# An encoder layer on one core: the last 512 tokens' down projection by seven block products

## The chip, the cores and the metric

The kernel runs on one core of a Trainium2 chip. The metric is the device time of one execution in microseconds (us). A core has a matrix engine (PE, with a separate stream PEld for loading stationary operands), a vector engine (DVE), a scalar engine (ACT), a third elementwise engine (POOL) and a queue engine (SP) that mostly issues transfers (DMAs) between the memory of the chip (HBM) and the core's own memories: SBUF for operands and PSUM, eight banks of 128 partitions x 512 floats, in which matmuls accumulate. Every engine works through its own instructions in order and waits on semaphores.

## What is computed

One layer of a hybrid encoder on 2048 tokens of width 1024 in float32; in front of the part that changes stand an attention over a dilated window, a convolution and a cross-attention. The projection of the values `v` is part of `w_in`; the MLP and the last norm are what the change is about.

```python
D_MODEL, SEQ, D_FF = 1024, 2048, 4096
y = rmsnorm(h, norm_mix_g[l]) @ w_in[l]            # q, k, v and the convolution's a, g
v = y[..., 2 * D_ATT:3 * D_ATT].reshape(B, S, ATT_HEADS, HEAD_DIM)
h = h + jnp.concatenate([att, conv], axis=-1) @ w_out[l]
...
h = h + xo @ w_xo[l]                               # cross-attention
u = rmsnorm(h, norm_mlp_g[l]) @ w_up[l]
h = h + jnp.square(jax.nn.relu(u)) @ w_down[l]
return rmsnorm(h, norm_final_g)
```

## The kernel before

**Numbers.** Every float32 operand of a matmul is split into a high part, rounded to the form that PE takes, and a low part, the rest. A product is three matmuls, high x high, low x high and high x low (`mm3`, L199 to L201). For weights, `wsplit2` does the split: ACT copies the raw tile to the high part (L190), DVE subtracts for the low part (L191). A weight tile of 512 KB (128 x 1024 floats) is loaded through `dma` (L57) on SP's queue into one of two buffers "raw"; there are four pairs of split buffers.

**Stages.** The first 540 us make projections; the last of these is `lin_v` (L548 on), in two rounds of two heads' groups: the raw weights times a scale (L560, DVE), cast (L562, ACT), low part (L563, POOL), then matmuls of 256 columns into PSUM, taken out by ACT (L574) and DVE (L575, `vst`), and stored to HBM (`vtok`). `weave` interleaves it with a convolution (`conv0`) on DVE. Then four passes of 512 tokens follow, p = 0 to 3; in each, `post(p)` makes the output projection, the cross-attention, the MLP and the final norm, with attention and convolution of the next pass woven in as sides. The last pass has no sides.

**The MLP of a pass.** h stays in SBUF transposed: eight tiles `hs[m]` of 128 features x 512 tokens. The 4096 hidden features come in eight groups (`fg`) of 512. In a group, four "up" steps c = 0 to 3 each make 128 hidden features x 512 tokens from one weight tile: 8 x 3 matmuls of 128x512. DVE takes the maximum with zero and the norm's scale (`rl`, L1321), ACT squares (L1322) and casts (`hhh`, L1323), DVE makes the low part (`hhl`, L1324). Four "down" steps follow, each with one weight tile (4 x 128 hidden features x 256 outputs) and two outputs' blocks of 4 x 3 matmuls of 128x512, added to `hs[m]` by DVE (L1339). So a group has 96 matmuls up and 96 down. Weights are the stationary operand in both, tokens the moving one. Up and down share three PSUM banks.

**The end.** In the last group of the last pass the down steps run on 256 tokens at a time (192 matmuls of 128x256), with squares summed beside them (`add_sq`, L1164, L1165). `final` takes the norm's factor (a matmul with ones `nps`, L1174; DVE L173; a power on POOL, L177; three DVE steps L178 to L180), multiplies by the gain (`fin`, L1360), turns blocks of 128x128 with PE (`ot`, L1367), scales on the way out of PSUM (L1369 on ACT, L1371 on DVE) and stores each half row block.

The order in which instructions stand on each engine is made by a scheduler from the program's order, from what `weave` interleaves and from priorities (`pinned`).

Of the kernel before, what the change touches and what calls it, by code (L numbers as in the profile page):

```python
# [10 lines left out]
F32 = mybir.dt.float32  # L11
# [36 lines left out]
def hybrid_layer(ctx, tc, A, out):  # L48
# [70 lines left out]
    bscr = dr.tile([KC, P, KC, P], F32, name="bscr")  # L119

# [77 lines left out]
    def mm3(o, lh, ll, rh, rl, first, end):  # L198
        PE.matmul(o, lh, rh, start=first, stop=False)  # L199
        PE.matmul(o, lh, rl, start=False, stop=False)  # L200
        last["pe"] = PE.matmul(o, ll, rh, start=False, stop=end)  # L201
# [1017 lines left out]
    def post(p):  # L1219
# [88 lines left out]
        end = p == NG - 1  # L1308
        for fg in range(FG):
# [16 lines left out]
            if fg == FG - 1:  # L1326
                fsum = ssum_tile(f"f{p}")
                if not end:
                    load_cat(p + 1, 0)

            def down(mp2, t, w, wh, wl):
                sl = slice(t, t + w)
                for e in range(2):
                    m = 2 * mp2 + e
                    es = slice(P * e, P * e + P)
                    pt = ps("mm", "dn")[:, 0:w]
                    for k in range(4):
                        mm3(pt, wh[:, k, es], wl[:, k, es], hh["h", k][:, sl], hh["l", k][:, sl], k == 0, k == 3)
                    last["dve"] = DVE.tensor_tensor(hs[m][:, sl], hs[m][:, sl], pt, op=ALU.add)  # L1339
                    if fg == FG - 1:  # L1340
                        add_sq(hs[m][:, sl], fsum[:, sl], m == 0)

            wd = []
            for mp2 in range(4):
                wd.append(wpost(wcols(w_down, mp2 * 256, 256, (4 * fg, 4 * fg + 4)), f"d{p}{fg}_{mp2}", (P, 4, 256)))
                if fg == FG - 1 and end:
                    continue
                down(mp2, 0, 512, *wd[-1])
                yield


        fin = {}

        def final(t, w):
            r = rstd_from(fsum[:, t:t + w])
            sl = slice(t, t + w)
            for k in range(KC):
                if t == 0:
                    fin[k] = ytile("h", k, f"fin{p}_{k}", F32)
                DVE.tensor_scalar(fin[k][:, sl], hs[k][:, sl], gain("final", k), None, op0=ALU.mult)  # L1360
            for j in range(w // P):
                c0 = t + P * j
                for g in range(2):
                    ot = ytile("l", 2 * (c0 // P) + g, f"ot{p}{c0}{g}", F32)
                    pt = ps("T", "ot")
                    for i in range(4):
                        PE.transpose(pt[:, P * i:P * i + P], fin[4 * g + i][:, c0:c0 + P], ident)  # L1367
                    if g:
                        ACT.activation(ot, pt, AF.Copy, scale=r[:, j:j + 1])  # L1369
                    else:  # L1370
                        DVE.tensor_scalar(ot, pt, r[:, j:j + 1], None, op0=ALU.mult)  # L1371
                    dma(out[0, 512 * p + c0:512 * p + c0 + P, 512 * g:512 * (g + 1)], ot)
                yield

        if end:
            for t in range(0, 512, 256):
                for mp2 in range(4):
                    down(mp2, t, 256, *wd[mp2])
                yield from final(t, 256)
        else:  # L1380
            load_cat(p + 1, 1)
            yield from final(0, 512)

    for p in range(NG):
# [8 lines left out]
        if p + 1 < NG:  # L1393
# [3 lines left out]
            sides = [(att(p + 1), 0.95), (cg, 0.6)]  # L1397
# [60 lines left out]
```

## Time and profile before

| | us |
|---|---|
| median of three runs | 2888.64 |
| lowest, highest | 2881.66, 2890.31 |
| the profiled execution | 2888.26 |
| its span, from the first to the last instruction | 2886.5 |
| busy time of PE in it | 2826.6 (98%) |
| busy time of DVE | 1857.6 (64%) |
| busy time of ACT | 1166.3 (40%) |
| mean granted PE clock | 0.994 |

The profile is of one execution. A row of a timeline has the start and the length in us, the engine, the line, the operation and its tiles, and in brackets the idle time before it and what ended it. A row of a group has the count, the busy time in us, the mean length of one in ns, the idle time before the group's instructions and what ended most of it. A line of the view of windows has, for a stretch, the busy time and count of PE, PEld, DVE, ACT and POOL, then PE's granted clock (1.00 is full), the mean busy share of the DMA engines and the GB/s they moved. A line of the waits has what waited for what, the sum in us, how often, and the longest.

### The profile page before, as it was taken

What the parts mean: (1) busy time and instruction counts of PE and PEld (TensorE: products, weight loads), DVE (VectorE), ACT (ScalarE), POOL (GpSimd) and SP (SyncE); (2) the same over time, 40 slices, a digit from 0 to 9 for tenths busy, and PEclk for the clock granted to TensorE, in tenths of its full rate; (3) what the DMA queues carried; (4) which work ended last, traced back from release to release, by engine and by line L of the source; (5) the groups of instructions that cost most, each with busy time, mean ns of one, the idle gap of its engine ahead of it and who ended that gap; (6) DMA issues with size and microseconds to landing.
All of it is one profiled execution on the core that took longest, in us unless ns stands there. A gap on an engine that the chain in (4) does not pass through costs nothing.

```text
span 2886.5 us, 41313 instructions
## 1 busy us (share of the span) xinstructions
PE 2826.6 (98%) x15628; PEld 2376.2 (82%) x15628; DVE 1857.6 (64%) x3306; ACT 1166.3 (40%) x1988; POOL 458.0 (16%) x469
## 2 busy tenths in 40 slices
PE   8999999998999999999999999999999999999999
PEld 7878899887788888888888888888888888888887
DVE  5636535565789776557887765689876555544445
ACT  5633211475554333434543343444333433432233
POOL 1336421122102011200012012002011200000000
PEclk9999999999999999999999999999999999999999
DMA  8979845799734444554444446534543445333332
GB/s 264 295 173 228 202 132 131 182 256 247 205 102 131 135 133 123 168 160 145 121 130 130 138 117 192 175 96 128 142 127 109 139 132 175 93 90 101 96 95 74
DMA packets 598632, 433.74 MB, mean 150 GB/s; under 512 B 191550, under 2 KB 524786, under 8 KB 597921
## 3 DMA queue, kind: packets, MB, share of 16 engines
q1 hardware_dynamic: 558256, 408.21, 50.2%
q10 hardware_dynamic: 37952, 16.88, 2.4%
q0 software_dynamic: 2224, 6.01, 0.6%
q8 instruction: 123, 2.02, 0.3%
q14 instruction: 77, 0.62, 0.1%
HBM read 339.89 MB, written 91.11 MB: 149 GB/s over the span
## 4 chain that ended last, share of the span: by engine, by line
PE 82%; DVE 9%; DMA 5%; issue 2%; ACT 2%; POOL 1%; SPq 1%; POOLq 0%; DVEq 0%; ACTq 0%
PE dn L199 8%; PE dn L200 8%; PE dn L201 8%; PE up L199 7%; PE up L200 7%; PE up L201 7%; PE lin L199 4%; PE lin L201 4%; PE lin L200 4%; DVE cacc L216 3%; PE o L199 2%; PE o L200 2%; PE o L201 2%; PE xs L199 2%; PE xs L201 2%; PE xs L200 2%
## 5 line engine op out<-in xcount | busy, mean ns | idle before, releaser
L199 PE MATMUL dn<-hhh,whi_d 128*128 128x512 f32 (+1 forms) x1056 | 402.8, 392 | 7.2 <-DVE h L1339 6.1
L200 PE MATMUL dn<-hhl,whi_d 128*128 128x512 f32 (+1 forms) x1056 | 403.4, 385 | 1.1 <-DVE hhl L1324 1.1
L199 PE MATMUL up<-mh,whi_u 128*128 128x512 f32 x1024 | 402.9, 393 | 0.5 <-DVE rl L1321 0.5
L201 PE MATMUL dn<-hhh,wlo_d 128*128 128x512 f32 (+1 forms) x1056 | 402.6, 384 | 0.0
L200 PE MATMUL up<-ml,whi_u 128*128 128x512 f32 x1024 | 399.4, 390 | 1.0 <-DVE ml L1214 0.9
L201 PE MATMUL up<-mh,wlo_u 128*128 128x512 f32 x1024 | 399.7, 391 | 0.0
L216 DVE SCALAR_TENSOR_TENSOR cacc<-cu,cw,cacc 128x512 f32<-128x512 f32 x480 | 389.0, 811 | 5.5
L190 ACT CAST whi_d<-raw_d 128x1024 fp32r<-128x1024 f32 x128 | 134.6, 1052 | 418.1 <-PE up L200 378.6
L1339 DVE TENSOR_TENSOR h<-h,dn 128x512 f32<-128x512 f32 (+1 forms) x264 | 172.3, 667 | 162.9 <-PE dn L201 161.7
L190 ACT CAST whi_u<-raw_u 128x1024 fp32r<-128x1024 f32 x128 | 134.4, 1050 | 327.2 <-PE dn L200 304.1
L1321 DVE SCALAR_TENSOR_TENSOR rl<-up,ssumx 128x512 f32<-128x512 f32 x128 | 88.0, 690 | 256.9 <-PE up L201 252.6
L199 PEld LDWEIGHTS dn<-hhh,whi_d 128*128 128x128 f32 x1056 | 198.1, 189 | 47.5 <-DVE h L1339 10.2
L201 PEld LDWEIGHTS dn<-hhh,wlo_d 128*128 128x128 f32 x1056 | 198.8, 188 | 39.7
L200 PEld LDWEIGHTS dn<-hhl,whi_d 128*128 128x128 f32 x1056 | 199.3, 189 | 37.4 <-DVE hhl L1324 2.0
L200 PEld LDWEIGHTS up<-ml,whi_u 128*128 128x128 f32 x1024 | 192.4, 188 | 40.1 <-DVE ml L1214 2.3
L201 PEld LDWEIGHTS up<-mh,wlo_u 128*128 128x128 f32 x1024 | 192.2, 188 | 40.3
L199 PEld LDWEIGHTS up<-mh,whi_u 128*128 128x128 f32 x1024 | 192.4, 188 | 38.5 <-DVE rl L1321 0.9
L774 ACT ACTIVATE sm<-sm,o 128x256 f32<-128x256 f32 (+1 forms) x384 | 160.1, 466 | 126.3 <-DVE o L773 125.9
L773 DVE CUSTOM_DVE_ANT_0 sm<-s,mask 128x256 f32<-128x256 f32 (+1 forms) x384 | 128.5, 375 | 83.5 <-PE s L999 39.4
L191 DVE TENSOR_TENSOR wlo_u<-raw_u,whi_u 128x1024 fp32r<-128x1024 f32 x128 | 158.4, 1237 | 32.7 <-ACT whi_u L190 32.4
L191 DVE TENSOR_TENSOR wlo_d<-raw_d,whi_d 128x1024 fp32r<-128x1024 f32 x128 | 163.2, 1275 | 23.8 <-ACT whi_d L190 23.7
L177 POOL TENSOR_TENSOR nr<-st_v,mhalf 128x4 f32<-128x4 f32 (+1 forms) x13 | 13.0, 997 | 839.2 <-DVE st_v L173 839.2
(403 smaller groups left out, 6320.9 us busy)
## 6 DMA issues: line engine op xcount, KB each, us to landing
raw_u<-in_w_up_dram SPq DMA_DIRECT2D x128, 512.0 KB
raw_d<-in_w_down_dram SPq DMA_DIRECT2D x128, 512.0 KB
raw_o<-in_w_out_dram SPq DMA_DIRECT2D x32, 512.0 KB
raw_a<-ascr SPq DMA_DIRECT2D x32, 512.0 KB
raw_b<-bscr SPq DMA_DIRECT2D x32, 512.0 KB
k<-kscr SPq DMA_DIRECT2D x24, 512.0 KB
k<-kscr SPq DMA_DIRECT2D x8, 1152.0 KB
xn<-in_x_dram SPq DMA_DIRECT2D x32, 256.0 KB
```

Source lines behind the costliest of these rows:

```text
L177: POOL.tensor_tensor(dst, v, mhalf.to_broadcast([P, v.shape[1]]), op=ALU.pow)
L190: ACT.copy(hi, raw)
L191: (lo_eng or DVE).tensor_tensor(lo, raw, f(hi), op=ALU.subtract)
L199: PE.matmul(o, lh, rh, start=first, stop=False)
L200: PE.matmul(o, lh, rl, start=False, stop=False)
L201: last["pe"] = PE.matmul(o, ll, rh, start=False, stop=end)
L216: DVE.scalar_tensor_tensor(acc, u[:, t:t + 512], cw[:, c, t:t + 1], acc, op0=ALU.mult, op1=ALU.add)
L773: last["dve"] = DVE.tensor_tensor_reduce(dst, so, mask[:, 256 * m:256 * m + nk], 1.0, 3e38, ALU.add, ALU.min, mn)
L774: last["act"] = ACT.activation(dst, dst, AF.Exp, bias=mn, scale=-1.0)
L1321: last["dve"] = DVE.scalar_tensor_tensor(r, pt, 0.0, rsb, op0=ALU.max, op1=ALU.mult)
L1339: last["dve"] = DVE.tensor_tensor(hs[m][:, sl], hs[m][:, sl], pt, op=ALU.add)
```

## The change

In the last pass the function `last_mlp` takes the place of the MLP, and `down_sums` makes sums of weights ahead of it.

- For groups 0 to 6 the down projection is turned: stationary is the hidden activation (128 features x 128 tokens), moving are 512 columns of weights, and the result is 128 tokens x 512 outputs, added by DVE to h kept by rows of tokens. A group's product of (512 tokens x 512 features) with (512 features x 1024 outputs) is cut into 2 x 2 blocks, and seven products of blocks (A11, A12, S2, S1, S3, S4, A22; Winograd's form of Strassen's scheme) take the place of eight. Each is 2 x 2 x 3 = 12 matmuls of 128x512.
- The accumulators X, Y and Z of PSUM are read by DVE after each product that adds to them, and X and Z are accumulated further afterwards (`more`). X has banks 0 and 1, Y and Z share banks 2 and 3, and the up steps get 4 to 7.
- `parts` makes the activations' blocks and their sums S1 to S4, each split in two, on DVE and ACT.
- Of the seven weight tiles of a group, three are read from `w_down` and four, sums of blocks, from `dscr` in HBM, each as two DMAs of 256 KB; with the four up tiles there are eleven tiles a group for eight.
- `down_sums` fills `dscr`: for each of 7 groups, 4 m and 2 j a unit of two loads of 128x256 floats (SP's queue), four DVE subtractions of 128x128 in place, and two stores (ACT's queue). Groups 0 to 3 are woven beside `lin_v`, groups 4 to 6 given to the last pass as a side.
- h is turned into rows during the first two up steps of group 0 (32 transposes, 8 ACT copies); the 32 transposes behind the norm go.
- Group 7 has its down projection by rows without the seven products: for each of four row blocks and two halves 4 x 3 matmuls of 128x512. The first up step of the next group stands ahead of the seven products.
- The final norm goes row block by row block: ACT squares and sums along the row, DVE and POOL make the factor, DVE multiplies by factor and gain in one step (two per row block), and the two halves are stored from SP's and ACT's queue.

```diff
+    dscr = dr.tile([7, 4, P, 4, 256], F32, name="dscr")
...
+    def down_sums(pl, tag, fgs):
+        for fg, m, j in ((fg, m, j) for fg in fgs for m in range(4) for j in range(2)):
+            raw = pl.tile([P, 2, 256], F32, tag=tag, name=f"ds{fg}{m}{j}", bufs=2)
+            for a in range(2):
+                k = 4 * fg + 2 * a + j
+                dma(raw[:, a], w_down[P * k:P * k + P, 256 * m:256 * m + 256])
+            yield
+            (b11, b12), (b21, b22) = ([raw[:, a, P * b:P * b + P] for b in range(2)] for a in range(2))
+            for o, x, y in ((b11, b12, b11), (b12, b22, b12), (b22, b22, b11), (b21, b21, b22)):
+                last["dve"] = DVE.tensor_tensor(o, x, y, op=ALU.subtract)
+            for a in range(2):
+                dma(dscr[fg, m, :, 2 * a + j], raw[:, a], nc.scalar)
...
-        for _ in range(4):
-            next(steps)
-        weave(islice(steps, 8), (conv0, 1))
-        for _ in range(4):
-            next(steps)
+        ds = pinned(down_sums(pool("dsum", stack=st), "ds", range(4)), "dve")
+        weave(islice(steps, 4), (ds, 2))
+        weave(islice(steps, 8), (conv0, 1), (ds, 2))
+        weave(islice(steps, 4), (ds, 2))
+        drain(ds)
         weave(steps, (conv0, 2.2))
...
+    def last_mlp(hs, y, rsb):
+        FG, p = 8, NG - 1
+        banks.update(up=(4, 5, 6, 7), ux=(0, 1), uy=(2, 3), tr=(0, 1, 2, 3))
...
+        def parts(rs_, c):
+            r, j = rs_[c], c % 2
+            lo, hi = r[:, 0:256], r[:, 256:512]
+            if c < 2:
+                split([x[:, j] for x in A1], lo)
+                DVE.tensor_tensor(lo, lo, hi, op=ALU.subtract)
+                split([x[:, j] for x in S3], lo)
+            else:
+                r0 = rs_[j]
+                split([x[:, j] for x in A2], r)
+                DVE.tensor_tensor(r0[:, 256:512], r0[:, 256:512], hi, op=ALU.add)
+                DVE.tensor_tensor(r0[:, 0:256], hi, r0[:, 0:256], op=ALU.subtract)
+                split([x[j] for x in S12], r0)
+                DVE.tensor_tensor(lo, lo, r0[:, 0:256], op=ALU.subtract)
+                split([x[:, j] for x in S4], lo)
+        def seven(fg):
...
+            X, Y, Z = ([ps(kind, "dn") for _ in range(2)] for kind in ("ux", "uy", "uy"))
+            for n, (key, w, pts, more, t0, c0) in enumerate((
+                    ("A11", direct(0, 0), X, False, 0, 0), ("A12", direct(1, 0), Y, False, 0, 0),
+                    ("S2", sums(1, 1), X, True, 0, 1), ("S1", sums(0, 0), Z, False, 2, 1),
+                    ("S3", sums(0, 1), X, True, 2, 1), ("S4", direct(1, 1), Z, True, 0, 1),
+                    ("A22", sums(1, 0), X, True, 2, 0))):
+                raw = wp.tile([P, 2, 512], F32, tag="raw", name=f"raw_d{p}{fg}{n}", bufs=2)
+                for j in range(2):
+                    dma(raw[:, j].rearrange("p (m c) -> p m c", m=4), w[j])
...
+                wh, wl = wsplit2(wq if i % 4 > 1 else wp, raw, f"d{p}{fg}_{n}", shape=(P, 2, 512))
+                for t in range(2):
+                    for j in range(2):
+                        mm3(pts[t], at[key](0, j, t), at[key](1, j, t), wh[:, j], wl[:, j], not more and j == 0, j == 1,
+                            more)
+                    a = row(t0 + t).rearrange("p (m h c) -> p m h c", m=4, h=2)[:, :, c0, :]
+                    last["dve"] = DVE.tensor_tensor(a, a, pts[t].rearrange("p (m c) -> p m c", m=4), op=ALU.add)
+        rs_ = []
+        for fg in range(FG - 1):
+            for c in range(4):
+                if c or not fg:
+                    rs_.append(hidden(fg, c))
+                parts(rs_, c)
+            rs_ = [hidden(fg + 1, 0)]
+            seven(fg)
...
+        for t in range(4):
+            for c in range(2):
+                pt = ps("tr", "dn")
+                for k in range(4):
+                    wh, wl = ws[c][k // 2]
+                    mm3(pt, *(x[:, k, P * t:P * t + P] for x in hh), wh[:, k % 2], wl[:, k % 2], k == 0, k == 3)
+                a = row(t)[:, 512 * c:512 * c + 512]
+                DVE.tensor_tensor(a, a, pt, op=ALU.add)
+                ACT.activation(tmp("sq"), a, AF.Square, accum_out=ss[:, 2 * t + c:2 * t + c + 1])
...
+            rstd_col(r[:, 0:1], sq, 1, top)
+            for c in range(2):
+                a = row(t)[:, 512 * c:512 * c + 512]
+                DVE.scalar_tensor_tensor(a, a, r[:, 0:1], grow[:, 512 * c:512 * c + 512], op0=ALU.mult, op1=ALU.mult)
+                dma(out[0, 512 * p + P * t:512 * p + P * (t + 1), 512 * c:512 * c + 512], a, nc.scalar if c else None)
...
+        else:
+            sides = [(down_sums(kq, "k", range(4, 7)), 1.2)]
         weave(main, *sides)
```

More of the change, by code (lines that the diff above doesn't have):

```diff
@@ L1349, in post @@
                 yield
+        load_cat(p + 1, 1)
+        r = rstd_from(fsum)
         fin = {}
-        def final(t, w):
-            r = rstd_from(fsum[:, t:t + w])
-            sl = slice(t, t + w)
-            for k in range(KC):
[L1358 to L1382, printed above, removed]
+        for k in range(KC):
+            fin[k] = ytile("h", k, f"fin{p}_{k}", F32)
+            DVE.tensor_scalar(fin[k], hs[k], gain("final", k), None, op0=ALU.mult)
+        for j in range(4):
+            c0 = P * j
+            for g in range(2):
+                ot = ytile("l", 2 * j + g, f"ot{p}{c0}{g}", F32)
+                pt = ps("T", "ot")
+                for i in range(4):
+                    PE.transpose(pt[:, P * i:P * i + P], fin[4 * g + i][:, c0:c0 + P], ident)
+                if g:
+                    ACT.activation(ot, pt, AF.Copy, scale=r[:, j:j + 1])
+                else:
+                    DVE.tensor_scalar(ot, pt, r[:, j:j + 1], None, op0=ALU.mult)
+                dma(out[0, 512 * p + c0:512 * p + c0 + P, 512 * g:512 * (g + 1)], ot)
+            yield
```

88 lines of the change are left out of this document (70 added, 18 removed).

## The prediction

> **What bounds the kernel now.** I read the page from the top: span, engines, the chain that ended last; then the last pass by groups of equal shape; then single rows.
>
> ```profile
> span 2886.5 us, 41313 instructions
> PE 2826.6 (98%) x15628; PEld 2376.2 (82%) x15628; DVE 1857.6 (64%) x3306; ACT 1166.3 (40%) x1988; POOL 458.0 (16%) x469
> PE 82%; DVE 9%; DMA 5%; issue 2%; ACT 2%; POOL 1%; SPq 1%; POOLq 0%; DVEq 0%; ACTq 0%
> 2400.00:2700.00 300.00, 298.80 (x1345) 245.79 (x1344) 155.69 (x221) 107.22 (x159) 2.01 (x2) 1.00 0.35 106
> ```
>
> TensorE sets the time: 98% of the span, 298.8 of 300 us in the last pass's MLP (columns of the last line: length, then busy time of PE, weight loads, DVE, ACT, POOL, granted clock, DMA share, GB/s). DVE is busy 52% there and the clock is full. So a matmul less in this stage is time, as long as DVE, ACT and the weight loads keep pace with fewer matmuls.
>
> What is a matmul worth? The grouped rows give a mean of 389 ns, but that is a latency: rows overlap, and the distance of the starts counts.
>
> ```profile
> L200 PE MATMUL dn<-hhl,whi_d 128*128 128x512 f32 x108 | 41.6, 389 | 0.0
> 2835.05 0.39 PE L199 MATMUL up<-mh,whi_u 128*128 128x512 f32 x1
> 2835.28 0.39 PE L200 MATMUL up<-ml,whi_u 128*128 128x512 f32 x1
> ...
> 2837.77 0.39 PE L199 MATMUL up<-mh,whi_u 128*128 128x512 f32 x1
> 2869.24 0.28 PE L200 MATMUL dn<-hhl,whi_d 128*128 128x256 f32 x1
> 2869.36 0.28 PE L201 MATMUL dn<-hhh,wlo_d 128*128 128x256 f32 x1
> ...
> 2869.84 0.60 PE L1367 MATMUL ot<-ident,fin 128*128 128x128 f32 x4
> 2870.19 0.36 PE L199 MATMUL dn<-hhh,whi_d 128*128 128x256 f32 x1
> ```
>
> Twelve starts lie between 2835.05 and 2837.77: 2.72/12 = 0.2267 us for 512 columns. 256 columns take 0.12, four transposes 0.35.
>
> **The term that shrinks.** In groups of hidden features 0 to 6 (of 8), 96 down matmuls become seven products of 12, so 84: 7 x 12 x 0.2267 = **-19.0 us**. (By the 389 ns it would be 32.7, which would be wrong.)
> The Trainium skill, "TensorE: Matmul & The Clock Gate", "Wait — 56ns, not 53.3ns?", has warm matmuls start every 215.7 ns at 512 columns; the measured distance is 5% longer, and by the page the term would be 18.1 us.
>
> **The end of the pass.**
>
> ```profile
> 2850.47 0.39 PE L201 MATMUL up<-mh,wlo_u 128*128 128x512 f32 x1
> 2850.69 0.28 PE L199 MATMUL dn<-hhh,whi_d 128*128 128x256 f32 x1
> ...
> 2878.70 0.70 POOL L177 TENSOR_TENSOR nr<-st_v,mhalf 128x2 f32<-128x2 f32 x1 [10.40 <-DVE st_v L173]
> 2879.43 0.16 DVE L178 TENSOR_TENSOR st_t<-nr 128x2 f32<-128x2 f32 x1 [0.81 <-POOL nr L177]
> ...
> 2882.36 0.75 DVE L1371 TENSOR_SCALAR ot<-ot,nr 128x512 f32<-128x512 f32 x1 [1.59 <-PE ot L1367]
> ```
>
> From the first down matmul of group 7 (2850.69) to the span's end (2886.5) pass 35.8 us: half-width matmuls, 32 transposes, the norm, the output. The last output is ready at 2883.11, so its transfer closes the span 3.4 us later. After the change: 96 x 0.2267 = 21.8 us, then for the last row block an add (0.69), a square with its sum (0.62 and some 0.2, estimated), a sum and a variance (0.16 each), POOL's power (0.81 with its hand-over), three small operations (0.6), two scalings (1.4), 3.4 for the output and some 0.5 of hand-overs: 8.5. Together 30.3: **-5.5**. The 32 transposes are not gone but turn h into rows in group 0: 8 x 0.35 = **+2.8**. Their four banks are emptied by eight ACT copies, and ACT is at 36% there; with the copies late, the second four groups would wait, up to 3 us.
>
> In group 7 the down matmuls now stand right behind the last up:
>
> ```profile
> 2703.51 0.69 DVE L1321 SCALAR_TENSOR_TENSOR rl<-up,ssumx 128x512 f32<-128x512 f32 x1 [3.35 <-PE up L201]
> 2704.24 0.62 ACT L1322 ACTIVATE rl<-rl 128x512 f32<-128x512 f32 x1
> 2704.89 0.62 ACT L1323 CAST hhh<-rl 128x512 fp32r<-128x512 f32 x1
> ```
>
> From rl's start to the end of the split (another 0.69 on DVE) 2.8 to 2.9 us; nine matmuls on earlier features cover 2.0: **+1** (0 to 2).
>
> **The seven products: do the others keep pace?** Per product PE needs 2.72 us. Rows of the same work:
>
> ```profile
> L191 DVE TENSOR_TENSOR wlo_d<-raw_d,whi_d 128x1024 fp32r<-128x1024 f32 x16 | 19.6, 1226 | 2.7 <-ACT whi_d L190 2.7
> L1339 DVE TENSOR_TENSOR h<-h,dn 128x512 f32<-128x512 f32 x28 | 18.7, 686 | 37.2 <-PE dn L201 37.2
> L190 ACT CAST whi_d<-raw_d 128x1024 fp32r<-128x1024 f32 x16 | 16.9, 1054 | 56.0 <-PE up L200 56.0
> L1339 DVE TENSOR_TENSOR h<-h,dn 128x256 f32<-128x256 f32 x16 | 6.6, 420 | 3.3 <-PE dn L201 2.9
> ```
>
> DVE: two adds and one split, 2 x 0.686 + 1.226 = 2.60 of 2.72 us: it just fits, and what is late in the products is caught up in the ups (5.44 us each). Over a whole group DVE has some 22 operations of 512, 14 of 256 and 11 splits: 15.1 + 5.9 + 13.5 = 34.5 of 40.8 us. A PSUM bank that is read between two accumulations is written again only one product later (the order X, Y, X, Z, X, Z, X), so an add may come 2.7 us late before PE stands.
>
> The weights, a load for each 2.72 us instead of 5.44:
>
> ```profile
> 2698.92 1.23 DVE L191 TENSOR_TENSOR wlo_u<-raw_u,whi_u 128x1024 fp32r<-128x1024 f32 x1 [0.17 <-ACT whi_u L190]
> 2703.28 1.05 ACT L190 CAST whi_d<-raw_d 128x1024 fp32r<-128x1024 f32 x1 [4.39 <-PE up L200]
> 2702.50:2703.00 0.50, 0.50 (x4) 0.42 (x3) 0.00 (x0) 0.00 (x0) 0.00 (x0) 1.00 1.02 360
> 2703.00:2703.50 0.50, 0.50 (x4) 0.42 (x3) 0.00 (x0) 0.22 (x1) 0.00 (x0) 1.00 0.26 88
> ```
>
> A raw buffer is free at 2700.15 and its 512 KB are in at about 2703.2, so 3.1 us; with cast and split 5.5 for one of two buffers, 2.75 per weight. That is PE's pace, but four split pairs are full when the products begin, so the last weight is still made some 5 us ahead of its use. I take **+1** for all seven groups (0 to 14, 2 us a group, if DVE's order puts a split behind a waiting add).
>
> **The sums of weights** are what the change pays. 56 units: two loads of 128 KB on SP's queue, four 128x128 subtractions on DVE, two stores from ACT's queue, two buffers. From 0.686 for 512 and 0.420 for 256 elements a subtraction costs an estimated 0.285, a unit 1.14 on DVE; 32 units beside the values' projection make 36.5 us, 24 more 27.4.
>
> In the instruction order of the changed kernel the 24 stand in the third pass (its groups 4 to 6), ahead of the last pass. DVE there:
>
> ```profile
> 2220.00:2240.00 20.00, 20.00 (x116) 16.30 (x115) 16.41 (x26) 8.12 (x13) 7.01 (x6) 1.00 0.34 93
> 2240.00:2260.00 20.00, 20.00 (x109) 16.85 (x109) 9.85 (x18) 7.59 (x12) 1.39 (x1) 1.00 0.36 111
> ```
>
> 26 of 40 us are taken (66%); 27.4 us spread over the some 90 us of three groups add 30%, so DVE is nearly full, and hidden parts stand in its order behind subtractions that wait for loads. I take **+2.5** (0 to 10).
>
> The values' projection is the open place:
>
> ```profile
> 440.00:460.00 20.00, 20.00 (x91) 16.47 (x90) 6.10 (x8) 4.10 (x5) 3.82 (x4) 1.00 0.15 46
> 460.00:480.00 20.00, 20.00 (x164) 19.80 (x163) 12.67 (x20) 3.44 (x8) 7.32 (x8) 1.00 0.78 204
> 388.30 1.21 DVE L560 TENSOR_TENSOR raw_v<-raw_v,vbc 128x1024 f32<-128x1024 f32 x1
> 456.42 1.22 DVE L560 TENSOR_TENSOR raw_v<-raw_v,vbc 128x1024 f32<-128x1024 f32 x1
> 457.67 1.05 ACT L562 CAST wvh<-raw_v 128x1024 fp32r<-128x1024 f32 x1 [5.08 <-DVE raw_v L560]
> 458.79 2.39 POOL L563 TENSOR_TENSOR wvl<-raw_v,wvh 128x1024 fp32r<-128x1024 f32 x1 [3.73 <-ACT wvh L562]
> L199 PE MATMUL v<-wvh,xh x256: 277/283/283, 393.0 to 506.8; 128*128 128x256 f32 x128
> 467.35 0.36 SPq L57 DMA_DIRECT2D vtok<-vst  x1
> 470.82 0.11 POOL L572 MEMSET vst<- 128x8 f16 x1 [1.76 <-DMA vtok<-vst]
> ```
>
> DVE has room (6 to 13 of 20 us), but it works in order, and between the two multiplications of raw_v at 388.30 and 456.42 stand 19 units: each must take no more than 68/19 = 3.6 us, or the second comes late, and behind it ACT's cast, POOL's 2.39 us and the values' matmuls, with no slack. A unit: its load 2.2 to 3.1 us (3.1 for 512 KB above; half of that is the stream), 1.14, its store 2.2 to 3.5 (the 130 KB stored from 467.35 release POOL at 470.82): 5.5 to 7.7 for each of two buffers, 2.8 to 3.9 per unit. Then ten units beside the second half of the projection (its matmuls end at 507), where the DMA engines were 78% busy already, hold up the evacuations (vst) behind them. At 2.8 nothing is lost; at 3.9, 19 x 0.3 + 3. One wait may vanish in exchange:
>
> ```profile
> PE lin L199 <- DVE vst L575: 3.1, 1, 3.1
> ```
>
> I take **+4** (-3 to +9).
> The Trainium skill, "DMA: Bandwidth & Descriptors", speaks against these transfers: "Anatomy of one DMA" gives every DMA about 2.0 us plus bytes at 436 GB/s, most of it the receipt of the write, heaviest in HBM, and "Bandwidth" advises 1 MiB or more. By it, an estimate, a 128 KB transfer takes 2.3 us and a unit 2.9, which is near the lower bound of the rows.
>
> **Sum** against the profiled run, 2888.3 us (1.8 of them outside the span; the median of the runs is 2888.6, 0.3 more): -19.0 - 5.5 + 2.8 + 1 + 1 + 2.5 + 4 = -13.2, **2875 us**.
>
> **Rivals.** (a) *The sums hide wholly*, loads and stores at the lower bounds: without the 6.5, 2868 to 2869; at best, with the 3.1 of the vanished wait, 2865. For it: DVE's idle time; against: waits in order.
> (b) *The sums eat most of the gain*: both places at their upper bounds, +9 and +10 for 6.5, so 2887, between 2880 and 2895. For it: the 78% DMA share from 460 on; against: a late DVE is caught up where PE has several banks ahead.
> (c) *DVE paces the seven products.* An add reads its PSUM and a strided half of a row; if it costs 0.95 instead of 0.69, a product takes 3.13 and not 2.72: 49 x 0.41 = 20 us, 2895 less what the ups catch up, some 2888. It decides from (2.72 - 1.23)/2 = 0.75 us per add. Against: the 128x512 add is 0.686 in 28 cases.
> (d) *Slower than before: the units set the pace of the projection.* If a buffer's cycle is 10 us, because the stores in HBM come back late behind the projection's own traffic, a unit takes 5 us and 32 need 160, where the projection has 120 (388 to 507): +40 for my +4, 2911. Over the bound of 2897 it comes from a cycle of about 9.1 us on; the rows give at most 7.7.
> (e) The change does not do what it says: PE's order shows 84 matmuls per group, so I give it nothing.
>
> **How the numbers follow.** What a measurement of this kernel can tell from no change is about 0.3%, 8.7 us: faster is under 2880, slower over 2897. Chances: the forecast 0.50 (its own range 2869 to 2881), (a) 0.10, (b) 0.20, (c) 0.08, (d) 0.12. Faster: nearly all of the forecast, (a) and a little of (b), 0.62; slower: (d) and the ends of (b) and (c), 0.14; the same 0.24. The range, 2864 to 2893, leaves out (d) and some of the edges.
>
> **What would show it.** Steps: seven groups of 84 matmuls at 0.2267 us, so about 40.8 us per group; the span's end some 30 us behind the last up; no idle PE with an add's or a split's name in the seven; PE waits of the values' projection (about 388 to 510) and of the third pass's last groups longer by 6 or 7 us together, named after vst, wvl, hhl or rl, with subtractions ahead of them on DVE. Wrong it would be if a unit takes over 4 us, if the adds take over 0.75, or if the last pass shows PE waits of more than 2 us in each group.

## The result and the profile after

| | us |
|---|---|
| before, median of 5 runs | 2888.64 |
| after, median of 5 runs (2928.04 to 2938.66) | 2935.26 |
| after, the profiled execution's span | 2936.9 |
| ratio after / before, 95% interval | 1.0165 (1.0143 to 1.0186) |
| forecast, with its range | 2875 (2864 to 2893) |

The change costs 46.6 us where 13 were to be won. The page of the profile after, and its view of PE's waits:

```profile
span 2936.9 us, 41990 instructions
PE 2850.7 (97%) x15440; PEld 2366.5 (81%) x15440; DVE 1999.5 (68%) x3669; ACT 1204.2 (41%) x2055; POOL 455.5 (16%) x471
PE 73%; DMA 11%; DVE 10%; issue 2%; SPq 2%; ACT 1%; POOL 0%; ACTq 0%; DVEq 0%; POOLq 0%
L761 DVE TENSOR_TENSOR ds<-ds 128x128 f32<-128x128 f32 x224 | 80.2, 364 | 96.5 <-DMA ds<-in_w_down_dram 79.8
```

```profile
PE vbc L186 <- DVE raw_v L562: 11.3, 1, 11.3
PE lin L201 <- DVE vst L577: 10.5, 2, 10.2
PE dn L201 <- DVE h L1356: 7.3, 3, 2.5
...
PE dn L202 <- DVE hhl L1343: 5.1, 4, 2.9
```

The chain that ended last now has 11% DMA where it had 5%; the units' subtractions (ds) sat 80 us waiting for their own loads; two waits of over 10 us stand at the values' projection. But one number doesn't fit a story of waits alone: PE has 188 matmuls fewer (15440 for 15628) and is busy 24 us *longer* (2850.7 for 2826.6). The next view is of windows of 200 us in the last pass, before and after:

```profile
2640.00:2840.00 200.00, 200.00 (x880) 164.55 (x879) 94.04 (x111) 58.72 (x72) 0.00 (x0) 1.00 0.33 98
```

```profile
2640.00:2840.00 200.00, 200.00 (x869) 162.92 (x868) 153.96 (x228) 91.03 (x123) 0.00 (x0) 1.00 0.48 140
```

At full clock and with PE busy throughout, 200 us hold 869 matmuls instead of 880. The rows of one up step of the profile after say the same:

```profile
2657.65 0.39 PE L201 MATMUL up<-mh,whi_u 128*128 128x512 f32 x1
2657.88 0.40 PE L202 MATMUL up<-ml,whi_u 128*128 128x512 f32 x1
2658.11 0.39 PE L203 MATMUL up<-mh,wlo_u 128*128 128x512 f32 x1
...
2663.02 0.39 PE L203 MATMUL up<-mh,wlo_u 128*128 128x512 f32 x1
```

From the first of these rows to the last there are 23 distances (from the start of one matmul to the start of the next) in 5.37 us: 0.2335 us where the prediction counted 0.2267. In both profiles I took all distances of 512-column matmuls: from 1000 us on the mean is 227.8 ns before and 231.1 after, and the distances differ by as much between 100 and 370 us, where nothing in the code has changed yet. So there are at least two losses: waits around the sums, and a slower PE in the whole program.

### The profile page after: what moved, and what is told of

The parts are those of the page before. It is cut to its first block, busy times and chain, and to the rows that moved or that the text cites. A ratio compares the mean times of both kernels' runs of the same rounds, so it can differ in the third digit from the quotient of the medians.

```text
span 2936.9 us, 41990 instructions
## 1 busy us (share of the span) xinstructions
PE 2850.7 (97%) x15440; PEld 2366.5 (81%) x15440; DVE 1999.5 (68%) x3669; ACT 1204.2 (41%) x2055; POOL 455.5 (16%) x471
## 4 chain that ended last, share of the span: by engine, by line
PE 73%; DMA 11%; DVE 10%; issue 2%; SPq 2%; ACT 1%; POOL 0%; ACTq 0%; DVEq 0%; POOLq 0%
PE dn L201 7%; PE dn L202 7%; PE dn L203 7%; PE up L201 7%; PE up L202 7%; PE up L203 7%; DMA ds<-in_w_down_dram 3%; DMA dscr<-ds 3%; PE lin L201 3%; PE lin L203 3%; PE lin L202 3%; DVE cacc L218 3%; PE o L201 2%; PE o L202 2%; PE xs L201 2%
## 5 line engine op out<-in xcount | busy, mean ns | idle before, releaser
L201 PE MATMUL dn<-hhh,whi_d 128*128 128x512 f32 x768 | 304.3, 406 | 12.1 <-DVE h L1356 7.3
L202 PE MATMUL dn<-hhl,whi_d 128*128 128x512 f32 x768 | 305.9, 401 | 5.1 <-DVE hhl L1343 5.1
L203 PE MATMUL dn<-hhh,wlo_d 128*128 128x512 f32 x768 | 304.1, 398 | 0.0
L192 DVE TENSOR_TENSOR wlo_d<-raw_d,whi_d 128x1024 fp32r<-128x1024 f32 x149 | 187.6, 1259 | 38.3 <-ACT whi_d L191 38.0
L1356 DVE TENSOR_TENSOR h<-h,dn 128x512 f32<-128x512 f32 x192 | 128.5, 682 | 80.2 <-PE dn L203 79.8
L201 PEld LDWEIGHTS dn<-hhh,whi_d 128*128 128x128 f32 x768 | 145.3, 190 | 45.8 <-DVE h L1356 9.6
L202 PEld LDWEIGHTS dn<-hhl,whi_d 128*128 128x128 f32 x768 | 146.8, 191 | 36.7 <-DVE hhl L1343 7.3
L203 PEld LDWEIGHTS dn<-hhh,wlo_d 128*128 128x128 f32 x768 | 146.5, 191 | 33.1
L1340 DVE SCALAR_TENSOR_TENSOR rl<-up,ssumx 128x512 f32<-128x512 f32 x96 | 65.9, 689 | 150.3 <-PE up L203 150.1
L761 DVE TENSOR_TENSOR ds<-ds 128x128 f32<-128x128 f32 x224 | 80.2, 364 | 96.5 <-DMA ds<-in_w_down_dram 79.8
```

What stands on the lines that cost most here:

```text
L192: (lo_eng or DVE).tensor_tensor(lo, raw, f(hi), op=ALU.subtract)
L201: PE.matmul(o, lh, rh, start=first, stop=False, skip_group_check=more)
L202: PE.matmul(o, lh, rl, start=False, stop=False, skip_group_check=more)
L203: last["pe"] = PE.matmul(o, ll, rh, start=False, stop=end, skip_group_check=more)
L761: last["dve"] = DVE.tensor_tensor(o, x, y, op=ALU.subtract)
L1340: last["dve"] = DVE.scalar_tensor_tensor(r, pt, 0.0, rsb, op0=ALU.max, op1=ALU.mult)
```

## The experiments

### The cadence: where the operands lie in SBUF

Two small tiles that `last_mlp` takes from the pool `top` (the right-hand end of SBUF), which the excerpts of the change above don't show, move nearly every tile of the right-hand pools 96 bytes down. Two runs ask what that costs, with `tpad`, the first tile of that pool:

```diff
-    top.tile([P, 296], F32, name="tpad")
+    top.tile([P, 320], F32, name="tpad")     # e1: the kernel before; e2: the changed kernel with 272
```

> The kernel before with its first right-hand SBUF tile (tpad) 24 floats longer, so that nearly all tiles of the right-hand pools lie 96 bytes lower, as the two new small tiles of the change put them. Nothing else differs. Theory A (place): in the profile after, matmuls of 512 columns start every 231 ns from 100 us on, where the code is still the same as before, and 227 to 228 ns in the profile before; the places of the operands in SBUF set this, so this kernel takes about 10,700 x 3.2 ns = 34 us more than before: 2917 to 2927 us. Theory B (the sums or the run): the longer distance comes from the added transfers or from the execution; then this kernel takes 2885 to 2893 us and its starts lie 227 to 228 ns apart.

> The changed kernel with tpad 24 floats shorter, so that the right-hand tiles lie where they lay before. Theory A: the 34 us of the slower cadence go, 2935 - 34 = 2901 us (2896 to 2906), with the waits beside the values' projection and in the third pass as they were, about 21 us each. Theory B: 2930 to 2940 us.

e1: 2918.88 us, 1.0100 (1.0084 to 1.0115) of before: 29 us for 96 bytes. e2: 2917.32 us, 1.0100 (1.0083 to 1.0117), so 18 us of the change's 46.6 are the place. That is less than the 34 expected and the 29 of e1, and e2 lies outside the ranges of both theories. Why it is less isn't shown: the profiled spans of e1 and of the kernel before are 26 us apart, those of the changed kernel and of e2 23. The windows of e1 and e2:

```profile
2640.00:2840.00 200.00, 200.00 (x867) 162.00 (x866) 90.57 (x108) 59.12 (x74) 0.00 (x0) 1.00 0.31 95
```

```profile
2640.00:2840.00 200.00, 200.00 (x884) 165.59 (x883) 156.92 (x232) 91.93 (x124) 0.00 (x0) 1.00 0.50 144
```

The unchanged kernel, moved, does 867; the changed kernel, moved back, 884, as the kernel before did (880). Theory A holds as to the cause. Which matmuls are slow? Rows of e1 at a change from an up with weights in the right-hand pool to a down with weights in the left-hand pool:

```profile
2693.13 0.40 PE L200 MATMUL up<-ml,whi_u 128*128 128x512 f32 x1
...
2698.73 0.40 PE L200 MATMUL up<-ml,whi_u 128*128 128x512 f32 x1
...
2701.95 0.39 PE L199 MATMUL dn<-hhh,whi_d 128*128 128x512 f32 x1
...
2703.99 0.39 PE L199 MATMUL dn<-hhh,whi_d 128*128 128x512 f32 x1
```

24 distances in 5.60 us, 0.2333 us; then, after some more, nine in 2.04 us, 0.2267. The third and the last pass show it throughout: only steps whose weights have moved are slow, though the activations that stream past them (left-hand pool) lie where they lay. It doesn't matter which of the two operands has moved. Between 100 and 370 us of the profile after, the weights lie in the left-hand pool, and the matmuls whose activations lie in the right-hand one start 234 ns apart on average, the others 228. In the last pass of the changed kernel, where the weights move and the activations stand, the down steps with weights from the right take 234 ns, the others 228.

In the kernel before, weights and activations start 32 bytes past a multiple of 512 on both sides, by the addresses in the built program. Three more moves of the kernel before asked what counts:

```diff
-    top.tile([P, 296], F32, name="tpad")
+    top.tile([P, 328], F32, name="tpad")     # e8: 128 bytes lower; e9: 424, 512 bytes lower
```

```diff
+    top.tile([P, 320], F32, name="tpad")     # e10: right-hand tiles 96 bytes lower ...
     cst = pool("cst")
+    cst.tile([P, 160], F32, name="cpad")     # ... and left-hand tiles 416 bytes higher
```

> The kernel before with tpad 32 floats longer: right-hand tiles 128 bytes lower, where e1_before_shift had 96. If it is the remainder of the addresses by 128 bytes that counts (left-hand and right-hand tiles have 32 in the kernel before, right-hand tiles 64 in the changed kernel and in e1_before_shift): starts 227 to 228 ns apart, 2885 to 2893 us. If any move of the right-hand pools is harmful: 231 ns, 2917 to 2921 us.

> The kernel before with tpad 128 floats longer: right-hand tiles 512 bytes lower. In e1_before_shift and e8_before_shift128 the ups whose weights (whi, wlo) lie in the right-hand pool (address 448 and 416 by remainder of 512) start 233.3 and 232.5 ns apart, those whose weights lie in the left-hand pool (remainder 32) 226.7 to 227. Theory A2 (the remainder by 512, the length of one 128-float row of weights): 226.7 everywhere in the last pass, 2885 to 2893 us. Rival (any move of the right-hand weights is slow): 232 or more in c = 2 and 3, about 2910.

> The kernel before with the right-hand tiles 96 bytes lower and the left-hand tiles 416 bytes higher: weights on both sides, and the activations that move past them, have the remainder 448. If the relation of a matmul's two operands counts (both with the same remainder is fast): 226.7 ns everywhere, 2885 to 2893 us. If the remainder of the weights alone counts (32 is fast, 448 slow): 233 ns in all four ups of a group, about twice e1's loss, 2945 us.

| run | weights on the right, activations, past a multiple of 512 | us | ratio to before |
|---|---|---|---|
| before (medians beside these runs) | 32, 32 | 2887 to 2890 | |
| e1 | 448, 32 | 2918.88 | 1.0100 (1.0084 to 1.0115) |
| e8 (two runs) | 416, 32 | 2909.36 | 1.0075 (1.0053 to 1.0096) |
| e9 | 32, 32 (moved by 512) | 2886.57 | 0.9994 (0.9983 to 1.0004) |
| e10 | 448, 448 | 2886.21 | 0.9992 (0.9980 to 1.0003) |

The windows of e8 and e10:

```profile
2640.00:2840.00 200.00, 200.00 (x869) 162.70 (x868) 92.63 (x110) 58.82 (x73) 0.00 (x0) 1.00 0.31 95
```

```profile
2640.00:2840.00 200.00, 200.00 (x881) 164.77 (x880) 93.88 (x111) 59.75 (x73) 0.00 (x0) 1.00 0.32 98
```

My first rule (remainder by 128) fell with e8, which is slow with equal remainders by 128. e9 and e10 say that it is the relation of the two operands: a move by 512 bytes is harmless, and 448 with 448 is as fast as 32 with 32. A distance of 256 bytes was not tried.

### The sums: what the units cost, and the last pass without them

All following kernels have `tpad` at 272. e3 leaves out `down_sums` and takes blocks of `w_down` in the place of the sums, which have the same size, so its output is not the layer's; e4 leaves out the early units only (groups 0 to 3 take blocks).

```diff
             def sums(a, b):
-                v = dscr[fg].rearrange("m p k (h c) -> p k m h c", h=2)
-                return [v[:, 2 * a + j, :, b, :] for j in range(2)]
+                return direct(a, b)              # e4: for fg < 4 only
```

> As e2_after_pad, without down_sums: the four sums of a group are replaced by the same blocks of w_down, so this leaves out the sums of weights, in the same number and size of loads in the last pass. Theory A with the sums as the second cause: what is left is the gain of the seven products, the tail and the transposes, 2888.6 - 19.0 - 2.7 + 1 = 2868 us (2863 to 2873). Rival: the last pass itself loses (adds or weights late), then 2880 or more. Theory B: about 2935 - 43 = 2892.

> As e3_no_sums, but with the 24 units of groups 4 to 6 kept (they stand in the third pass); the 32 units beside the values' projection are left out, and groups 0 to 3 use the blocks of w_down. If the third pass's waits of the changed kernel (2.9 + 2.3 + 2.5 and smaller ones, about 11 us by the waits and up to 22 us by the start of the last pass's first hidden part against the MLP's start) are the units' price: 2868 + 11 to 22 = 2879 to 2890 us. If the units there cost little and the loss there was the cadence: 2870.

e3: 2859.88 us, 0.9897 (0.9880 to 0.9913). e4: 2884.23 us, 0.9980 (0.9970 to 0.9989). So the 24 late units cost 24 us, and the 32 early ones (e2 less e4) 33. (e3 is 3 us under the range that was expected; e4 is inside its own.) The rows of `rl` (each hidden step has one; the rows give the first and the last start of a group) of before, e3, e4 and e2; x32 are those of the last pass:

```profile
L1321 DVE SCALAR_TENSOR_TENSOR rl<-up,ssumx x128: 677/692/692, 911.0 to 2850.9; 128x512 f32<-128x512 f32 x128
L1321 DVE SCALAR_TENSOR_TENSOR rl<-up,ssumx x32: 681/692/692, 2538.5 to 2850.9; 128x512 f32<-128x512 f32 x32
```

```profile
L1340 DVE SCALAR_TENSOR_TENSOR rl<-up,ssumx x96: 677/692/693, 903.7 to 2353.9; 128x512 f32<-128x512 f32 x96
L1419 DVE SCALAR_TENSOR_TENSOR rl<-up,ssumx x32: 679/691/692, 2533.5 to 2830.9; 128x512 f32<-128x512 f32 x32
```

```profile
L1340 DVE SCALAR_TENSOR_TENSOR rl<-up,ssumx x96: 676/692/693, 907.3 to 2373.9; 128x512 f32<-128x512 f32 x96
L1419 DVE SCALAR_TENSOR_TENSOR rl<-up,ssumx x32: 679/691/692, 2553.2 to 2850.6; 128x512 f32<-128x512 f32 x32
```

```profile
L1340 DVE SCALAR_TENSOR_TENSOR rl<-up,ssumx x96: 677/692/692, 939.3 to 2407.4; 128x512 f32<-128x512 f32 x96
L1419 DVE SCALAR_TENSOR_TENSOR rl<-up,ssumx x32: 679/691/692, 2586.8 to 2884.2; 128x512 f32<-128x512 f32 x32
```

Read the first and the last start in the rows with x32: from the first to the last hidden step of the last pass it is 297.4 us in e3, e4 and e2, with sums or without, and 312.4 before. The last pass itself loses nothing by the sums. The early units show in the first row's start (939.3 for 907.3: 32 us before the first MLP), the late ones in the stretch from 903.7 or 907.3 to the last pass (1629.8 in e3, 1645.9 in e4: 16 us). That first start also moves without a cause in the code: 904 to 915 us in profiles of kernels that are alike up to there. So a difference of under 10 us needs the medians.

What PE loses is mostly waiting: up to the first hidden step PE idles 60.3 us in the profile of e2 and 36.6 in that of e4, and from there to the last pass 23.4 us in e4 and 11.7 in e3. In e4, in the stretch of the late units (2160 to 2440 us), it waits for hidden parts, where e3 has only 2.5 us, for `h`:

```profile
PE dn L201 <- ACT hhh L1342: 6.0, 4, 3.4
PE dn L201 <- DVE h L1356: 3.0, 2, 2.4
PE dn L202 <- DVE hhl L1343: 2.8, 3, 2.4
```

### Through whom the units cost

Early units alone, first without their stores (e6), then without their subtractions (e7); then with the stores issued by POOL instead of ACT (e13), and the loads as well (e17). e14 and e18 do the last two with the late units. In all six the last pass takes blocks of `w_down` in place of the sums left out or unused.

```diff
-            for o, x, y in ((b11, b12, b11), (b12, b22, b12), (b22, b22, b11), (b21, b21, b22)):
-                last["dve"] = DVE.tensor_tensor(o, x, y, op=ALU.subtract)      # e7
-                dma(dscr[fg, m, :, 2 * a + j], raw[:, a], nc.scalar)
+                                                                               # e6: no store
+                dma(dscr[fg, m, :, 2 * a + j], raw[:, a], nc.gpsimd)           # e13, e14, e17, e18
-                dma(raw[:, a], w_down[P * k:P * k + P, 256 * m:256 * m + 256])
+                dma(raw[:, a], w_down[P * k:P * k + P, 256 * m:256 * m + 256], nc.gpsimd)   # e17, e18
```

> As e3_no_sums with the 32 units beside the values' projection put back, without their stores (loads and subtractions alone; the result is not used). With the stores these units cost e2_after_pad minus e4_late_sums = 33 us, which would be about 2893. Theory C (the store's return holds the two buffers, and through them SP's queue, and ACT's queue holds its vst casts behind the stores): a buffer's cycle is a load and 1.14 us, 2.1 us a unit against 3.6 that the order allows, so 2862 to 2868 us. Theory D (DVE waits in order for loads; the store only adds): at least half of the 33 stays, 2877 or more.

> As e6_early_no_store, but with the stores and without the subtractions (loads and stores alone). If the delay reaches PE through DVE, which waits in order at a subtraction for its load (42.9 us of waits beside the projection in the profile of e2_after_pad): 2862 to 2868 us. If it reaches PE through ACT, whose queue holds a store until its data are there and the vst casts behind it (39.7 + 37.8 us of waits in the same view): 2880 to 2893.

> The 32 units beside the values' projection as in the changed kernel (loads, subtractions, stores; the sums are not used, the last pass takes the blocks of w_down), with the stores issued by POOL in place of ACT. With ACT's queue these units cost 33 us (e2_after_pad less e4_late_sums), about 2893. If ACT's place in the chain is the price (77 us of waits of vst casts behind stores in e2_after_pad; e7_early_no_sub lost 30 without a subtraction): 2862 to 2874 us, near e6_early_no_store. If SP's queue and DVE, which wait for the stores' return all the same, pass it on: 2885 or more.

> As e13_early_poolq (2893 us) with the units' loads, too, issued by POOL, so that neither SP's nor ACT's queue holds anything for them. If SP's queue passed the price on (44 to 62 us of waits for the stores' return): 2862 to 2874 us. If DVE does, in order behind the loads (43 to 66 us of waits): 2885 or more.

> As e4_late_sums (24 units in the third pass, 2884 us) with the stores issued by POOL in place of ACT, where the casts of the MLP's weights waited 42 us for the units (whi_d and whi_u behind ds and dscr). If ACT's order is the price: 2862 to 2870 us. If DVE's (27 us more in two groups) or the queue SP's: 2880 or more.

> As e14_late_poolq (2887 us) with the units' loads issued by POOL. If SP's queue, where the loads of the MLP's weights stand behind the units' (59 us of waits for the stores' return), was the price: 2862 to 2870 us. If DVE: 2880 or more.

| early units | us | over e3 | late units | us | over e3 |
|---|---|---|---|---|---|
| as changed (e2 less e4) | | 33 | as changed (e4) | 2884.23 | 24 |
| no stores (e6) | 2873.70 | 14 | | | |
| no subtractions (e7) | 2889.91 | 30 | | | |
| stores from POOL (e13) | 2893.12 | 33 | stores from POOL (e14) | 2886.89 | 27 |
| loads and stores from POOL (e17) | 2925.76 | 66 | loads and stores from POOL (e18) | 2874.91 | 15 |

These runs were measured in several batches, in which the kernel before has medians of 2886.9 to 2889.7 us. So the columns "over e3" are good to some 3 us.

DVE's arithmetic is not the price: without a subtraction 30 of 33 us stay. Without the stores 14 stay, between the two theories. ACT alone is not it either: I held it for the cause after e7, where PE waited 12.2 us for a cast that stood behind a store, and e13 and e14 refute that. The waits beside the projection, of PE in e7 and of PE, SP's queue and DVE in e13:

```profile
PE v L201 <- ACT wvh L564: 12.2, 1, 12.2
```

```profile
PE vbc L186 <- DVE raw_v L562: 8.1, 1, 8.1
SPq L57 <- DMA dscr<-ds: 44.2, 21, 4.0
DVE ds L761 <- DMA ds<-in_w_down_dram: 66.0, 40, 6.2
```

With the stores off ACT the same delay comes in through DVE, which stands 66 us at subtractions whose loads are late because SP's queue waits for the stores' return. I read this as the round trip of a unit (load, subtract, store, and the buffer free again), laid through whichever in-order queue; taken off one queue it shows on the next. For the late units SP's queue carries about half: e18 saves 12 us over e14 and lies between its two expectations. For the early ones the same step costs 33 us more. POOL has work of its own in its order there, and PE's longest wait in e17 is for that, so e17 says nothing for or against DVE:

```profile
PE s L874 <- POOL ql L813: 16.9, 1, 16.9
```

A unit's own pace is not the whole price. From one load into a buffer to the next, e6 takes 6.2 us on average and e7 7.2 (the 19 units between the second and the fourth multiplication of raw_v), both within the 5.5 to 7.7 of the prediction, and they cost 14 and 30 us all the same. Among the late units e18 takes 15.2 us and e14 12.6, and e18 is the faster run. That fits a price that lies in the other work that stands behind a waiting unit in the same queue.

Contention among the transfers is a rival that no run here separates: e7 and e13 move the same bytes as e2. Against it speaks that the DMA engines' share is 0.50 in the 20 us in which PE waits longest (460 to 480 us of the profile after), and that e14 and e18, with equal bytes, differ by 12 us. How e13's 33 us divide between SP and DVE stays open. A larger number of buffers was not tried.

### The sums without units

In passes 0 to 2 the raw tile of a down step holds just the four blocks that the sums need. e5 subtracts in place there and stores the tile: no loads, 28 stores of 512 KB.

```diff
+        parts = wsplit2(wq if n % 4 > 1 else wp, raw, name, shape=shape)
+        if sums is not None:
+            fg, m = sums
+            (b11, b12), (b21, b22) = ([raw[:, 2 * a:2 * a + 2, P * b:P * b + P] for b in range(2)] for a in range(2))
+            for o, x, y in ((b11, b12, b11), (b12, b22, b12), (b22, b22, b11), (b21, b21, b22)):
+                last["dve"] = DVE.tensor_tensor(o, x, y, op=ALU.subtract)      # e12, e16: POOL.tensor_tensor
+            dma(dscr[fg, m], raw)
...
+                                 (fg, mp2) if fg < FG - 1 and RIDE[fg] == p else None))
+    RIDE = (0, 1, 2, 0, 1, 2, 2)          # e5, e12; e11: (0, 0, 0, 0, 1, 2, 2); e15, e16: (fg + mp2) % 3 == p
```

> As e2_after_pad, but the sums of weights are made without units of their own: in the passes p = 0 to 2 the raw tile of a down step (512 KB, already in SBUF for the MLP) is turned into its four sums in place by four DVE subtractions of 2x128 elements, and stored with one DMA of 512 KB from SP's queue; groups 0 and 3 in pass 0, 1 and 4 in pass 1, 2, 5 and 6 in pass 2. 28 stores, no load, 28 x 4 x 0.42 = 47 us of DVE over 4,900 us of four engines' time. If the units' round trips (a load waited for by DVE, a store waited for by SP's queue and ACT) were what cost 33 and 24 us, little is left: 2860 + 0 to 8 = 2860 to 2868 us. If DVE's work itself was the price (47 us here for 64 us there): 2860 + some 35 = 2895.

> As e5_ride with another share of the groups: 0 to 3 in pass 0, 4 in pass 1, 5 and 6 in pass 2. In e5_ride, against e3_no_sums, the sums cost 1.6 and 2.8 us in groups 0 and 3 of pass 0, about 7 in group 1 of pass 1 and in group 2 of pass 2, 2 in group 4 of pass 1 and nothing in groups 5 and 6. If pass 0 is the cheap place: 2860 + 4 x 2 + 2 = 2870 us. If groups 1 and 2 cost 7 wherever they stand: 2881 again.

> As e5_ride with the subtractions on POOL (below 20% busy) in place of DVE (80 to 88% busy in the groups that lost). If DVE's order was what cost 20 us in e5_ride: 2860 + 0 to 6 = 2860 to 2866 us. If it is the raw tile that stays occupied (the weights' loads then come late): POOL is slower at it, so 2881 or more.

> As e5_ride (sums made in place in the raw tiles of the down steps, DVE), but tile m of group fg is taken in pass (fg + m) mod 3, so that no group holds more than two raw tiles longer. If the losses of e5 and e11 came from four tiles in a row held some 5 us longer each, more than the four pairs ahead can cover: 2860 + 0 to 6 = 2860 to 2866 us. If DVE's 47 us of work in the busy groups was the price: 2870 or more.

> As e15_spread with the subtractions on POOL. If four tiles in a row were the price: the same 2860 to 2866 us; if DVE's work in the busy groups is: 2860 to 2866 here and 2870 or more in e15.

| run | us | ratio to before |
|---|---|---|
| e5, whole groups, DVE | 2881.05 | 0.9974 (0.9961 to 0.9988) |
| e11, groups 0 to 3 in pass 0 | 2880.34 | 0.9973 (0.9962 to 0.9983) |
| e12, whole groups, POOL | 2879.51 | 0.9967 (0.9955 to 0.9980) |
| e15, one or two tiles a group, DVE | 2875.85 | 0.9958 (0.9944 to 0.9973) |
| e16, one or two tiles a group, POOL | 2874.78 | 0.9956 (0.9940 to 0.9972) |

All five are faster than both kernels, by 0.3 to 0.4% of the kernel before, and none reaches e3's 2860. e5 fits neither of its expectations; e11 points to groups 1 and 2 being dear in pass 0 as well, and e12, 1.5 us under "2881 or more", speaks against DVE's order as the price. Spreading the tiles gives some 5 us more by the medians, with intervals that overlap, and which engine subtracts makes 1 us, which is noise. So neither four tiles in a row nor DVE's work is the whole price: e15 and e16 were to be 2860 to 2866 by the first, and e16 by the second. What is left over e3, 15 us by the medians, is not explained; the profiled spans of e16 and e3 are 9 us apart, 5 of them ahead of the first MLP, where the code is the same, and 4 between it and the last pass.

```profile
L1347 DVE SCALAR_TENSOR_TENSOR rl<-up,ssumx x96: 674/692/693, 908.6 to 2362.8; 128x512 f32<-128x512 f32 x96
L1427 DVE SCALAR_TENSOR_TENSOR rl<-up,ssumx x32: 679/692/692, 2542.1 to 2839.6; 128x512 f32<-128x512 f32 x32
```

(2542.1 - 908.6 = 1633.5 for e3's 1629.8.)

## Why the prediction was wrong

By the medians: -30 (all but the sums, e3) + 24 (late units) + 33 (early units) + 18 (the place, after less e2) = 45 us, measured 46.6. These are steps from one run to the next, so they must add up (the rest is the spread of the kernel before, 2888.6 here and 2889.7 beside e3). The 33 holds with the late units present; no run has the early ones alone as changed.

- *The last pass* was right, in its mechanism and its size: -19.0 - 5.5 + 2.8 + 1 + 1 = -19.7 forecast. In e3 the hidden steps take 297.4 us for 312.4 (2850.9 less 2538.5), -15.0, and from the last `rl` to the span's end 29.5 us for 35.6, -6.1: -21. A group takes 40.8 us (the first `rl` of group 4 less that of group 3 in e3: 2673.15 - 2632.35), as forecast; DVE, at 78%, and the weights kept pace; an add took 0.68 us where rival (c) needs 0.75, and PE waited 0.5 us in all between 2540 and 2831 us. That e3's median wins 30 and not 21 I can't place: 5 us of it stand ahead of the last pass, where profiles of like code differ by as much.
- *A matmul at 0.2267 us* was the step that failed without being seen as one: the prediction took the distance as a property of the instruction. It is one of the instruction and of where its two operands lie, and the change moved one of them. The sum had no term for that: it cost 18 us here and 29 alone (e1). In the whole diff it is only two more tiles in `top`.
- *The early units, +4 (up to +9)*, is the term most wrongly sized: 33. Rival (d) had the place and the pace, though not the reason. Between the second and the fourth multiplication of raw_v, rows of DVE after,

```profile
393.34 1.22 DVE L562 TENSOR_TENSOR raw_v<-raw_v,vbc 128x1024 f32<-128x1024 f32 x1
...
478.08 1.21 DVE L562 TENSOR_TENSOR raw_v<-raw_v,vbc 128x1024 f32<-128x1024 f32 x1
```

  stand the same 19 units, now in 84.7 us: 4.5 us each and 8.9 per buffer, over the forecast's bound of 7.7 and over the 4 us per unit that the prediction named as a sign of being wrong. Means over these units, in us:

| | load issued to first subtraction | subtractions | to the second store's issue | to the next load into the buffer | cycle |
|---|---|---|---|---|---|
| prediction | 2.2 to 3.1 | 1.14 | not counted | 2.2 to 3.5 | 5.5 to 7.7 |
| profile after | 3.1 | 2.6 | 0.5 | 2.8 | 8.9 |

  So on average loads and stores came back within the bounds, and stores late in HBM, the reason that rival (d) gives, are not what these means show. The sum was wrong in the subtractions. One of them takes 0.29 us in the median, as estimated, but DVE does them in order with the convolution and `vst` between, and waits for the second load. The sum also left out the issue of the stores in ACT's order. By the sum of rival (d) this pace makes 32 x 4.46 - 120 = 23 us of the 33, but e7, whose cycle is 7.2, costs 30 as well. What the prediction left out beside the pace is that ACT's casts, the loads in SP's queue and DVE's next multiplication all wait while a unit waits. The price that the prediction takes from the Trainium skill ("DMA: Bandwidth & Descriptors", "Anatomy of one DMA"), 2.9 us a unit, is also too low for the 4.5 measured; that section gives its 2.0 us for transfers that POOL issues, and these are issued by SP and ACT. SP's queue alone waited 61 us in 27 waits for stores to return:

```profile
SPq L57 <- DMA dscr<-ds: 60.6, 27, 6.5
```

  PE then paid a second time, if little. After the long wait its first matmuls are 0.43 us apart where they were 0.23 before it:

```profile
473.09 0.48 PE L186 MATMUL vbc<-ident,vmul 128*128 128x128 f32 x1 [11.33 <-DVE raw_v L562]
473.22 0.77 PE L202 MATMUL lin<-xl,whi_a 128*128 128x512 f32 x1
...
475.07 0.63 PE L203 MATMUL lin<-xh,wlo_a 128*128 128x512 f32 x1
475.50 0.63 PE L201 MATMUL lin<-xh,whi_a 128*128 128x512 f32 x1
...
477.09 0.40 PE L202 MATMUL lin<-xl,whi_a 128*128 128x512 f32 x1
473.30:476.60 3.30, 3.30 (x9) 2.62 (x9) 2.67 (x3) 0.81 (x1) 2.38 (x1) 0.50 0.30 103
460.00:480.00 20.00, 8.67 (x31) 6.65 (x30) 12.45 (x29) 2.91 (x4) 2.59 (x3) 0.74 0.50 159
```

  The granted clock (third from the end of the last two rows) shows it: 0.50 in those 3.3 us, 0.74 in the 20 us around them. The Trainium skill, "TensorE: Matmul & The Clock Gate", "Part 1", says that an idle window of about 3.4 us halves the clock until one busy window has passed; the trace agrees, with about 3.5 us of matmuls at half the clock after 11.3 us of idling. That second payment is under 2 us. The wait for `vst` that might vanish grew from 3.1 to 10.2 us.
- *The late units, +2.5 (up to +10)*: 24 by the medians, 16 by the profiles. That DVE would be nearly full was seen; that the loads of the MLP's weights stand in SP's queue behind the units' loads, which wait for a buffer, was not (12 us of it, e14 less e18). The other half is not attributed.

## What to carry to other kernels

The price of a matmul read from a trace held only for the addresses of that trace: after any change of pools, compare the distance of matmuls in a stretch that was not edited before looking at what was. Work put "beside" something cost here what its round trip held up in every in-order queue it touched, and not its busy time: ask of each queue what stands behind a waiting step, and don't stop at the sum of the steps. And before making a helper stream, look for a place where the data already lie in SBUF: the same sums without loads of their own turned 2917 us into 2875.

## What the hardware showed that was not expected

A matmul with a stationary operand of 128x128 and 512 moving columns of 4 bytes started every 226.7 ns in the last pass where both operands start at the same remainder of 512 bytes, and every 232.5 to 233.3 ns in the ups where they are 128 or 96 bytes off. About one per cent of the whole kernel's time hung on it (e1 and e8 against e9 and e10), with PE shown as fully busy and its clock as full in both cases. The 256-column matmuls of the last group do not show it: they start 0.12 us apart before and in e1.
